# A batch of y in one 64 KB run per partition, with its last six rows copied aside so that its buffer comes free early

## The chip, the cores and the metric

The kernel runs on one core of one Trainium2 chip. The metric is the device time of one execution in microseconds (us); runs of the same kernel agree within about 0.3%. All comparisons below are of undisturbed ("fast") runs. Data travel in **packets**, here one per partition of a load, 8 on each of 16 DMA engines. A load **lands** when its semaphore says that all of it is there; landings are read from the start of the instruction that waits, about 0.1 us later, where nothing else is said. A **period** is the time from one batch's y to the next.

## The reference

```python
B, N, D = 8, 4096, 512
gram = np.matmul(x, y.transpose(0, 2, 1))
diag = np.diagonal(gram, axis1=1, axis2=2)      # only x[b,n,:] . y[b,n,:] is needed
diag = diag - diag.max(axis=-1, keepdims=True)
exp = np.exp(diag)
return (exp / exp.sum(axis=-1, keepdims=True)).astype(np.float32)
```

So it is 8 x 4096 dot products of 512 elements, then a softmax of each batch's 4096 results. Both inputs (134.22 MB together) are read once.

## The kernel before

A batch has 32 rows in each of 128 partitions (R = 32), 64 KB of x and 64 KB of y per partition. There are two buffers for x and one for y. SyncE ("SP") issues the loads in program order. VectorE multiplies in place and reduces. Batches 0 to 5 are "wide" (large instructions), batches 6 and 7 go row by row, because at the end short pieces shorten what follows the last load.

```python
xs = [big.tile([P, R, D], f32, name=f"xs{i}") for i in range(2)]
ys = big.tile([P, R, D], f32, name="ys")
# load_x / load_y: one DMA of n rows from r0 on.  dots_wide: xs *= ys (VectorE).
# sums_wide: diag[:, b, :] = sum of xs over D (VectorE).  dot_row: one row, multiply and sum.

for b in range(wide):                    # wide = 6
    load_x(b, 0, R)
    for r0 in (0, R // 2):
        load_y(b, r0, R // 2)
        dots_wide(b, r0, R // 2)
    ...                                  # softmax of batches 0 to 4 in between
    sums_wide(b)

b = B - 2
load_x(b, 0, R)
for r0 in (0, R // 2):
    load_y(b, r0, R // 2)
    for r in range(r0, r0 + R // 2):
        dot_row(b, r)

b = B - 1
r0 = 0
for n in (8, 8, 8, 4, 2, 1, 1):
    load_x(b, r0, n)
    load_y(b, r0, n)
    for r in range(r0, r0 + n):
        ...                              # softmax of batches 5 and 6 in between
        dot_row(b, r)
    r0 += n
last_softmax(b)
```

## Time and profile before

| | before |
|---|---|
| time, median | 322.69 us (4 runs, 322.57 to 322.77) |
| span in the profile | 320.5 us |
| load queue | 134.22 MB, 97.4% of 16 engines' span |
| VectorE busy | 78% |
| a wide batch | 38.78 us, of which VectorE works 34.60 |

From the page of the kernel before: the DMA row in 40 slices (9 is 90% busy or more), the packets, the load queue, the chain that ended last, and the three large groups of VectorE (busy us, mean ns of one | idle us before them, and what ended it).

```profile
span 320.5 us, 318 instructions
...
DMA  9999999899999999989999999999999999999991
...
DMA packets 6113, 134.36 MB, mean 419 GB/s; under 512 B 1632, under 2 KB 1632, under 8 KB 2400
...
q1 hardware_dynamic: 5040, 134.22, 97.4%
q10 hardware_dynamic: 1072, 0.13, 0.3%
q14 instruction: 1, 0.01, 0.0%
...
DMA 77%; DVE 20%; issue 1%; SPq 0%; POOLq 0%; ACT 0%; POOL 0%; DVEq 0%; ACTq 0%
...
L55 DVE TENSOR_TENSOR xs<-xs,ys 128x8192 f32<-128x8192 f32 x12 | 104.3, 8692 | 53.6 <-DMA ys<-in_y_dram 53.6
L58 DVE TENSOR_REDUCE diag<-xs 128x32 f32<-128x16384 f32 x6 | 103.3, 17220 | 0.2
L62 DVE SCALAR_TENSOR_TENSOR xs<-xs,ys 128x512 f32<-128x512 f32 x64 | 40.0, 688 | 13.8 <-DMA ys<-in_y_dram 13.6
```

The load queue is full from end to end. VectorE waits for y (53.6 + 13.6 us), and no slice but the last, with the final softmax, shows the queue empty. The 20% that the chain puts on VectorE ("DVE") is the time until a multiply releases the issue of a load; that load then stands behind others in the queue, so this is no cost unless the queue runs empty.

One wide period in the timeline (start, duration; "SPq" is the issue of a load by SyncE):

```profile
42.00 8.69 DVE L55 TENSOR_TENSOR xs<-xs,ys 128x8192 f32<-128x8192 f32 x1 [0.94 <-DMA ys<-in_y_dram]
50.73 17.22 DVE L58 TENSOR_REDUCE diag<-xs 128x32 f32<-128x16384 f32 x1
67.97 0.33 SPq L48 DMA_DIRECT2D xs<-in_x_dram  x1
71.13 8.69 DVE L55 TENSOR_TENSOR xs<-xs,ys 128x8192 f32<-128x8192 f32 x1 [3.19 <-DMA ys<-in_y_dram]
79.85 9.97 SPq L51 DMA_DIRECT2D ys<-in_y_dram  x2
80.77 8.69 DVE L55 TENSOR_TENSOR xs<-xs,ys 128x8192 f32<-128x8192 f32 x1 [0.95 <-DMA ys<-in_y_dram]
```

From 42.00 to 80.77 is 38.77 us for one batch of 16.78 MB, 433 GB/s. Note the **lead** of the x load: it is issued at 67.97, and the queue's earlier loads (y of the next batch) have landed by 80.77, so the load is queued 12.8 us before the queue would run out.

### The profile page before, as it was taken

What the parts mean: (1) busy time and instruction counts of PE and PEld (TensorE: products, weight loads), DVE (VectorE), ACT (ScalarE), POOL (GpSimd) and SP (SyncE); (2) the same over time, 40 slices, a digit from 0 to 9 for tenths busy, and PEclk for the clock granted to TensorE, in tenths of its full rate; (3) what the DMA queues carried; (4) which work ended last, traced back from release to release, by engine and by line L of the source; (5) the groups of instructions that cost most, each with busy time, mean ns of one, the idle gap of its engine ahead of it and who ended that gap; (6) DMA issues with size and microseconds to landing.
All of it is one profiled execution on the core that took longest, in us unless ns stands there. A gap on an engine that the chain in (4) does not pass through costs nothing.

```text
span 320.5 us, 318 instructions
## 1 busy us (share of the span) xinstructions
DVE 248.9 (78%) x154; ACT 6.2 (2%) x26; POOL 3.3 (1%) x10
## 2 busy tenths in 40 slices
DVE  0000989969999689996899968998789969994494
ACT  1000000000000000000000000000101000010000
POOL 0000000000000000000000000000000000000000
DMA  9999999899999999989999999999999999999991
GB/s 393 393 393 458 429 421 523 348 438 491 425 393 429 421 458 401 515 364 421 515 401 393 442 409 458 450 401 450 401 523 393 394 448 407 425 429 427 421 410 59
DMA packets 6113, 134.36 MB, mean 419 GB/s; under 512 B 1632, under 2 KB 1632, under 8 KB 2400
## 3 DMA queue, kind: packets, MB, share of 16 engines
q1 hardware_dynamic: 5040, 134.22, 97.4%
q10 hardware_dynamic: 1072, 0.13, 0.3%
q14 instruction: 1, 0.01, 0.0%
HBM read 134.22 MB, written 0.13 MB: 419 GB/s over the span
## 4 chain that ended last, share of the span: by engine, by line
DMA 77%; DVE 20%; issue 1%; SPq 0%; POOLq 0%; ACT 0%; POOL 0%; DVEq 0%; ACTq 0%
DMA ys<-in_y_dram 74%; DVE xs L55 16%; DVE xs L62 4%; DMA out_dram<-res 3%; SPq L48 0%; POOLq L162 0%; ACT res L91 0%; POOL lmx L98 0%; DVE res L103 0%; DVE lmxp L97 0%; DVE lrc L102 0%; DVEq L55 0%; DVE brc L88 0%; DVEq L62 0%; DVEq L103 0%
## 5 line engine op out<-in xcount | busy, mean ns | idle before, releaser
L55 DVE TENSOR_TENSOR xs<-xs,ys 128x8192 f32<-128x8192 f32 x12 | 104.3, 8692 | 53.6 <-DMA ys<-in_y_dram 53.6
L58 DVE TENSOR_REDUCE diag<-xs 128x32 f32<-128x16384 f32 x6 | 103.3, 17220 | 0.2
L62 DVE SCALAR_TENSOR_TENSOR xs<-xs,ys 128x512 f32<-128x512 f32 x64 | 40.0, 688 | 13.8 <-DMA ys<-in_y_dram 13.6
L62 DVE DVE_READ_ACCUMULATOR xs<-xs,ys 128x1 f32 x64 | 5.3, 83 | 0.0
L77 ACT ACTIVATE anmx<-amx 128x5 f32<-128x5 f32 x1 | 0.2, 208 | 221.9 <-POOL amx L76 221.9
L76 POOL PARTITION_ALL_REDUCE amx<-amxp x1 | 0.4, 386 | 223.1 <-DVE amxp L75 223.1
L79 ACT ACTIVATE res<-diag,anmx 128x32 f32<-128x32 f32 x5 | 1.5, 309 | 0.0
L91 ACT ACTIVATE res<-res,arc 128x32 f32<-128x32 f32 x5 | 1.2, 309 | 19.0 <-DVE arc L88 19.0
L76 POOL PARTITION_ALL_REDUCE bmx<-bmxp x1 | 0.7, 736 | 60.5 <-DVE bmxp L75 60.5
L77 ACT ACT_TABLE_LOAD x1 | 1.3, 1283 | 0.7 <-PEq L151 0.7
L77 ACT ACTIVATE bnmx<-bmx 128x2 f32<-128x2 f32 x1 | 0.2, 203 | 41.6 <-POOL bmx L76 41.6
L79 ACT ACTIVATION_READ_ACCUMULATOR res<-diag,anmx 128x1 f32 x5 | 0.9, 187 | 0.0
L102 DVE RECIPROCAL lrc<-lssum 128x1 f32<-128x1 f32 x1 | 0.2, 162 | 1.0 <-POOL lssum L101 1.0
L83 POOL PARTITION_ALL_REDUCE bssum<-bsump x1 | 0.8, 797 | 1.1 <-ACT res L79 1.1
L100 ACT ACTIVATE res<-diag,lnmx 128x32 f32<-128x32 f32 x1 | 0.3, 321 | 19.6 <-DVE lnmx L99 19.6
L91 ACT ACTIVATE res<-res,brc 128x32 f32<-128x32 f32 x2 | 0.5, 313 | 8.0 <-DVE brc L88 8.0
L98 POOL PARTITION_ALL_REDUCE lmx<-lmxp x1 | 0.4, 367 | 26.7 <-DVE lmxp L97 26.7
L79 ACT ACTIVATE res<-diag,bnmx 128x32 f32<-128x32 f32 x2 | 0.6, 314 | 0.0
L99 DVE TENSOR_SCALAR lnmx<-lmx 128x1 f32<-128x1 f32 x1 | 0.2, 153 | 0.5 <-POOL lmx L98 0.5
L83 POOL PARTITION_ALL_REDUCE assum<-asump x1 | 0.5, 459 | 2.0 <-ACT res L79 2.0
L101 POOL PARTITION_ALL_REDUCE lssum<-lsump x1 | 0.4, 397 | 0.7 <-ACT res L100 0.7
L79 ACT ACTIVATION_READ_ACCUMULATOR res<-diag,bnmx 128x1 f32 x2 | 0.4, 188 | 0.0
(11 smaller groups left out, 1.9 us busy)
## 6 DMA issues: line engine op xcount, KB each, us to landing
ys<-in_y_dram SPq DMA_DIRECT2D x14, 4096.0 KB, 30.0
xs<-in_x_dram SPq DMA_DIRECT2D x3, 2048.0 KB, 19.5
ys<-in_y_dram SPq DMA_DIRECT2D x3, 2048.0 KB, 19.9
xs<-in_x_dram SPq DMA_DIRECT2D x1, 1024.0 KB, 26.6
ys<-in_y_dram SPq DMA_DIRECT2D x1, 1024.0 KB, 27.0
xs<-in_x_dram SPq DMA_DIRECT2D x1, 512.0 KB, 25.9
ys<-in_y_dram SPq DMA_DIRECT2D x1, 512.0 KB, 22.2
xs<-in_x_dram SPq DMA_DIRECT2D x2, 256.0 KB, 12.4
```

The source lines that it names most:

```text
L55: nc.vector.tensor_tensor(out=xt, in0=xt, in1=ys[:, r0 : r0 + n, :], op=Alu.mult)
L58: nc.vector.tensor_reduce(out=diag[:, b, :], in_=xs[b % 2], axis=X, op=Alu.add)
L62: nc.vector.scalar_tensor_tensor(out=xt[:, r, :], in0=xt[:, r, :], scalar=1.0, in1=ys[:, r, :], op0=Alu.mult, op1=Alu.mult, accum_out=diag ...
L76: nc.gpsimd.partition_all_reduce(out_ap=mx, in_ap=mxp, channels=P, reduce_op=bass_isa.ReduceOp.max)
L77: nc.scalar.mul(nmx, mx, -1.0)
L79: nc.scalar.activation(out=res[:, b0 + i, :], in_=diag[:, b0 + i, :], func=Act.Exp, bias=nmx[:, i : i + 1], scale=1.0, accum_out=sump[:, i ...
L83: nc.gpsimd.partition_all_reduce(out_ap=ssum, in_ap=sump, channels=P, reduce_op=bass_isa.ReduceOp.add)
L91: nc.scalar.activation(out=rb, in_=rb, func=Act.Copy, scale=rc[:, i : i + 1])
L98: nc.gpsimd.partition_all_reduce(out_ap=mx, in_ap=mxp, channels=P, reduce_op=bass_isa.ReduceOp.max)
L99: nc.vector.tensor_single_scalar(out=nmx, in_=mx, scalar=-1.0, op=Alu.mult)
L100: nc.scalar.activation(out=rb, in_=db, func=Act.Exp, bias=nmx, scale=1.0, accum_out=sump)
L101: nc.gpsimd.partition_all_reduce(out_ap=ssum, in_ap=sump, channels=P, reduce_op=bass_isa.ReduceOp.add)
```

## The change

Its intent: y comes in one run of 64 KB per partition instead of two of 32 KB, as x does. With one buffer for y, this would leave the next y waiting until the whole multiply is done. So ScalarE, which is idle, copies the last 6 rows of y aside; the main multiply covers 26 rows and frees y's place; the last 6 rows are multiplied from the copy. The last batch begins with one piece of 16 rows instead of two of 8 (and of 8, then 4, 2, 1, 1).

```diff
+    K = 6
+    side = big.tile([P, K, D], f32, name="side")
...
     for b in range(wide):
         load_x(b, 0, R)
-        for r0 in (0, R // 2):
-            load_y(b, r0, R // 2)
-            dots_wide(b, r0, R // 2)
+        load_y(b, 0, R)
+        nc.scalar.activation(out=side, in_=ys[:, R - K :, :], func=Act.Copy)
+        dots_wide(b, 0, R - K, ys[:, : R - K, :])
+        dots_wide(b, R - K, K, side)
...
-    for n in (8, 8, 8, 4, 2, 1, 1):
+    for n in (16, 8, 4, 2, 1, 1):
```

(`dots_wide` takes its second operand as an argument now; `...` marks what is left out.)

More of the change, by code (lines that the diff above doesn't have):

```diff
@@ L51, in load_y, with dots_wide @@
         nc.sync.dma_start(out=ys[:, r0 : r0 + n, :], in_=yv[b, :, r0 : r0 + n, :])
-    def dots_wide(b, r0, n):
+    def dots_wide(b, r0, n, yt):
         xt = xs[b % 2][:, r0 : r0 + n, :]
-        nc.vector.tensor_tensor(out=xt, in0=xt, in1=ys[:, r0 : r0 + n, :], op=Alu.mult)
+        nc.vector.tensor_tensor(out=xt, in0=xt, in1=yt, op=Alu.mult)
     def sums_wide(b):
```

## The prediction

> **What bounds it now.** The load stream. The DMA table gives 134.22 MB, 97.4% of 16 engines' span. In the timeline y's second halves release VectorE at 80.77, 119.55 and 158.33 us: one batch (16.78 MB) per 38.78 us, 432.6 GB/s. The Trainium skill, "DMA: Bandwidth & Descriptors", section "Specifications", gives 435 GB/s as the fabric ceiling; the trace agrees within 1%. VectorE works 34.60 us of each period (table by stage): 4 us of slack. The chain of waits names VectorE's first multiply (16%) only because it releases the issue of a y load, which then stands in a queue that is never empty. Outside the stream: the first DMA is issued at 0.72 us, eight batches at the steady rate take 310.2 us, the last piece lands at 314.97, the last row, softmax and store end at 320.5.
>
> **What the change does.** Bytes stay the same.
> - Removed per wide batch: two multiplies of 128x8192 (8.69 us each) and two y issues. Added: one y issue, multiplies of 13312 and 3072 elements (estimates from 1.061 ns per element: 14.12 and 3.26 us). With the 17.22 us reduction VectorE needs 34.65 us, as before.
> - ScalarE copies 3072 elements: estimate 2.8 us, from the Trainium skill, "ScalarE: Activation LUTs" (0.28 us + 0.833 ns per element); no such copy is in the trace. It ends long before the 14.12 us multiply, which therefore frees y.
> - With T the landing of y: the next x (19.4 us of stream) is already queued and streams from T to T+19.4. The next y is issued at T+14.2, 5 us ahead of its turn; the x after it at T+34.7, when the reduction ends, 4 us ahead of T+38.8. At the start, issue to steady flow plus landing cost about 2.5 us (first half lands at 32.26, against 29.1 us of stream), so both leads suffice, but x's shrinks from 12.8 us to 4.
> - VectorE starts a batch only when all of y is there, the first at 42 us instead of 32. That is slack, until batch 6: its rows run from 271 to 290 instead of 265 to 285. The last batch's first piece (16 rows) lands at 294 and is done at 304.3, just after the 8 rows land (303.8); 4, 2, 1, 1 fit what is left. The last row again waits for its own landing.
> - The large result store lands at about 299 (before 286), the second at 308; the load that reuses its completion semaphore is issued then, ahead of its turn at 313.
>
> **Sum.** Head, stream and tail stay. Packet length is the uncertain term: a y half in 32 KB packets comes in 9.64 us (435 GB/s), x in 64 KB packets plus a y half in 29.14 us, so x in 19.50 (430). If 64 KB costs this, six batches lose 0.2 us each: +1.2 us. Fewer pieces at the end give back a few tenths. None of the change's gain lies on the critical path: the queue never ran dry.
>
> Predicted 322.8 us, range 321.9 to 324.2; faster by over 2%: 0.01; within 2%: 0.95; slower: 0.04.
>
> **What would show it.** Right: batch period 38.7 to 39.0 us; VectorE waits for y once per batch, about 4 us, in place of 3.2 + 0.95; last piece lands at 314 to 316; ScalarE's copies take about 2.8 us.
> Wrong: a period over 39.3 us, with empty DMA slices around the start of an x load; y's issue waiting for ScalarE; the last loads waiting for result stores; VectorE behind in the last pieces.
>
> **What would make it wrong.** A lead that really needs over 4 us costs some us per batch. A 64 KB y run that streams faster gains at most about 1.5 us, to the 435 ceiling.

## The result

| | before | after |
|---|---|---|
| time, median | 322.69 us (4 runs) | 322.15 us (4 runs, 321.98 to 322.44) |
| ratio of fast runs | | 0.9985, 95% interval 0.9967 to 1.0002 |
| span in the profile | 320.5 us | 320.3 us |
| wide batch | 38.78 us | 38.73 us |
| last y piece lands | 314.97 us | 314.76 us |

A ratio is the mean time of one kernel's fast runs over that of the other's of the same rounds, so it is not quite the ratio of the medians. The change moved the time by at most a few tenths of a microsecond. The wide batch is the mean distance of the multiplies that start when a whole y has landed: (235.69 - 42.02) / 5 after, (235.88 - 42.00) / 5 before. In these two traces the last landing moves by only 0.21 us, less than the medians of the runs do.

The same lines of the page after:

```profile
span 320.3 us, 310 instructions
...
DMA  9999999999999999999999999999999999999991
...
DMA packets 4961, 134.36 MB, mean 419 GB/s; under 512 B 1504, under 2 KB 1504, under 8 KB 2272
...
q1 hardware_dynamic: 3888, 134.22, 97.3%
...
DMA 60%; DVE 36%; issue 2%; SPq 0%; POOLq 0%; ACT 0%; POOL 0%; DVEq 0%; ACTq 0%
...
L58 DVE TENSOR_TENSOR xs<-xs,ys 128x13312 f32<-128x13312 f32 x6 | 84.2, 14025 | 62.6 <-DMA ys<-in_y_dram 62.6
L61 DVE TENSOR_REDUCE diag<-xs 128x32 f32<-128x16384 f32 x6 | 103.3, 17220 | 0.2
...
L112 ACT ACTIVATE side<-ys 128x3072 f32<-128x3072 f32 x6 | 16.6, 2763 | 185.3 <-DMA ys<-in_y_dram 185.3
L58 DVE TENSOR_TENSOR xs<-xs,side 128x3072 f32<-128x3072 f32 x6 | 20.1, 3352 | 0.0
```

and the period in the timeline after:

```profile
41.95 2.76 ACT L112 ACTIVATE side<-ys 128x3072 f32<-128x3072 f32 x1 [39.94 <-DMA ys<-in_y_dram]
42.02 14.02 DVE L58 TENSOR_TENSOR xs<-xs,ys 128x13312 f32<-128x13312 f32 x1 [42.02 <-DMA ys<-in_y_dram]
55.97 3.35 DVE L58 TENSOR_TENSOR xs<-xs,side 128x3072 f32<-128x3072 f32 x1
56.13 0.33 SPq L54 DMA_DIRECT2D ys<-in_y_dram  x1
59.35 17.22 DVE L61 TENSOR_REDUCE diag<-xs 128x32 f32<-128x16384 f32 x1
76.60 0.33 SPq L51 DMA_DIRECT2D xs<-in_x_dram  x1
80.73 14.03 DVE L58 TENSOR_TENSOR xs<-xs,ys 128x13312 f32<-128x13312 f32 x1 [4.16 <-DMA ys<-in_y_dram]
```

Three things are to be seen. The DMA row is full to the end as before, with 1152 packets fewer in the load queue (5040 to 3888). VectorE's share of the chain rose from 20% to 36% while the time did not move, which is what a share of that chain is worth when the queue is full. And the leads shrank: x is issued at 76.60 for a queue that runs out at 80.73, 4.1 us ahead instead of 12.8; y is issued 14.1 us after its predecessor landed, 5.2 us before x lands (at 61.3).

### The profile page after: what moved, and what is told of

Same layout as the page of the kernel before. It is cut to its first block, busy times and chain, and to the rows that moved or that the text cites. A ratio compares the mean times of both kernels' runs of the same rounds, so it can differ in the third digit from the quotient of the medians.

```text
span 320.3 us, 310 instructions
## 1 busy us (share of the span) xinstructions
DVE 247.8 (77%) x154; ACT 22.7 (7%) x32; POOL 3.3 (1%) x10
## 3 DMA queue, kind: packets, MB, share of 16 engines
q1 hardware_dynamic: 3888, 134.22, 97.3%
## 4 chain that ended last, share of the span: by engine, by line
DMA 60%; DVE 36%; issue 2%; SPq 0%; POOLq 0%; ACT 0%; POOL 0%; DVEq 0%; ACTq 0%
DMA ys<-in_y_dram 57%; DVE xs L58 27%; DVE xs L65 5%; DVE diag L61 4%; DMA out_dram<-res 3%; POOLq L166 0%; ACT res L94 0%; SPq L51 0%; POOL lmx L101 0%; DVE res L106 0%; DVE lmxp L100 0%; DVE lrc L105 0%; DVE bmxp L78 0%; SPq L54 0%; DVEq L58 0%
## 5 line engine op out<-in xcount | busy, mean ns | idle before, releaser
L58 DVE TENSOR_TENSOR xs<-xs,ys 128x13312 f32<-128x13312 f32 x6 | 84.2, 14025 | 62.6 <-DMA ys<-in_y_dram 62.6
L112 ACT ACTIVATE side<-ys 128x3072 f32<-128x3072 f32 x6 | 16.6, 2763 | 185.3 <-DMA ys<-in_y_dram 185.3
L58 DVE TENSOR_TENSOR xs<-xs,side 128x3072 f32<-128x3072 f32 x6 | 20.1, 3352 | 0.0
```

What stands on the lines that cost most here:

```text
L58: nc.vector.tensor_tensor(out=xt, in0=xt, in1=yt, op=Alu.mult)
L112: nc.scalar.activation(out=side, in_=ys[:, R - K :, :], func=Act.Copy)
```

## The experiments

The theories that were put against each other:

- **A**: the load stream bounds; the change saves only the fixed part of packets.
- **B**: the early freeing of y is a gain, given back by VectorE's later start at the end.
- **C**: the leads matter; without the copy, or with less lead, loads would come too late. The prediction had put the need at about 2.5 us; before the first runs I lowered this to 1.5 us.
- **D**: packet length costs nothing.
- **E**: instruction fetches of VectorE share the load's engines and cost time.
- **F** and **G**, formed after the second set: a lead of about 2.5 us is enough (F), or any shortening costs in proportion (G).

| run | what differs | median us | ratio to before |
|---|---|---|---|
| e1_y_run_only | wide part of the change alone | 322.19 | 0.9982 |
| e2_pieces_only | last batch's pieces alone | 322.58 | 0.9997 |
| e3_no_side | changed, no copy aside | 331.53 | 1.0289 |
| e4_short_packets | changed, 16 KB packets | 324.58 | 1.0060 |
| e5_short_reduce | changed, most of the reduction cut | 321.80 | 0.9983 |
| e6_lead_2us | changed, x about 2.1 us ahead | 329.50 | 1.0229 |
| e7_lead_1us | changed, x about 1.0 us ahead | 328.36 | 1.0186 |
| e9_more_instr | changed, 256 tiny instructions more | 324.54 | 1.0066 |
| e10_lead_3us | changed, x about 3.1 us ahead | 325.71 | 1.0096 |
| e11_old_plus3us | before, 3.3 us more of VectorE | 322.54 | 1.0002 |
| e12_copy_2_rows | changed, 2 rows aside | 329.05 | 1.0188 |
| e13_one_memset | control for e9 | 322.19 | 0.9990 |

Before had medians of 322.68, 322.57 and 322.51 us in the three sets (e1 to e4, e5 to e9, e10 to e13). All results but that of e5 were correct. By the rule of 2% only e3 and e6 count as slower, and e7 and e12 are unclear; that all four are slower than before is clear of noise (the lowest of their intervals begins at 1.0136).

### The two halves of the change

e1 takes the changed kernel with the old pieces:

```diff
-    for n in (16, 8, 4, 2, 1, 1):
+    for n in (8, 8, 8, 4, 2, 1, 1):
```

> The wide batches as changed (y in one run, ScalarE's copy), the last batch in the old pieces 8, 8, 8, 4, 2, 1, 1. Theory A (the load stream bounds; the change saves only the fixed time of packets, about 8 to 9 ns each: a 32 KB packet takes 1213 ns and a 64 KB one 2418 in the traces, 2 x 1213 - 2418 = 8): each engine has 48 packets of 64 fewer, so 322.2 to 322.4, 0.3 to 0.5 us under before. Rival B (a gain of the early y is given back by VectorE's later start at the end): this run, which keeps the small first pieces, is under 321.8.

Measured: 322.19 us, ratio 0.9982 (0.9970 to 0.9994). e2 is the kernel before with the new pieces:

```diff
-    for n in (8, 8, 8, 4, 2, 1, 1):
+    for n in (16, 8, 4, 2, 1, 1):
```

> The old wide batches, the last batch in pieces 16, 8, 4, 2, 1, 1. Theory A: 16 packets per engine fewer, 322.5 to 322.7, at most 0.2 us under before. Rival B: over 323, because the larger first piece lets VectorE begin the last batch later.

Measured: 322.58 us, ratio 0.9997 (0.9985 to 1.0009). The small gain sits in the wide batches, the pieces are worth nothing measurable, and neither run shows a gain that the other part gives back: B falls.

### Packet length

e4 loads x and y of the wide batches of the changed kernel in pieces of 8 rows:

```diff
-        load_x(b, 0, R)
-        load_y(b, 0, R)
+        for r0 in range(0, R, 8):
+            load_x(b, r0, 8)
+        for r0 in range(0, R, 8):
+            load_y(b, r0, 8)
```

> The changed kernel with x and y of the wide batches loaded in pieces of 8 rows (16 KB packets) instead of whole: 64 packets per engine and batch instead of 16, six more loads per batch. Theory A at 8 to 9 ns a packet: 288 packets more per engine in six batches = 2.3 to 2.6 us, plus 0.3 us of completion packets (36 more of 9 ns): 324.6 to 325.2. Rival D (packet length costs nothing, the half us is something else, such as fewer loads or waits): 322.1 to 322.6.

Measured: 324.58 us (324.45 to 324.85), 2.4 us over the changed kernel; the period is 39.16 us instead of 38.73. That is at the lower end of what A gave, and D falls. In the packet records of the traces a packet takes 611 ns at 16 KB, 1213 at 32 KB and 2418 at 64 KB (medians): the time is proportional to the bytes, plus 8 to 9 ns (2 x 1213 - 2418 = 8, 2 x 611 - 1213 = 9). This also sizes the change itself. Each engine has 64 data packets fewer (4480 to 3456 in all, over 16) and 8 completion packets of 9 ns fewer; 64 x 8 + 8 x 9 ns = 0.6 us. The medians differ by 0.54 us. As the interval of the direct comparison includes 1, the gain itself rests on e1's interval and on this sum.

### Does VectorE's part cost anything?

e5 cuts the wide reductions to 32 of 512 elements per row:

```diff
-        nc.vector.tensor_reduce(out=diag[:, b, :], in_=xs[b % 2], axis=X, op=Alu.add)
+        nc.vector.tensor_reduce(out=diag[:, b, :], in_=xs[b % 2][:, :, 0:32], axis=X, op=Alu.add)
```

> The changed kernel with the wide reductions cut to 32 of 512 elements per row (a wrong result on purpose): about 16 us of VectorE's 34.6 us per batch are gone, and x is issued some 16 us earlier. Theory A (stream bounds, VectorE's 27% in the chain of waits is no cost): 321.9 to 322.3, unchanged. Rival C (the late issue of x, 4 us ahead, costs time): at least 1 us faster.

Measured: 321.80 us, ratio 0.9983 (0.9968 to 0.9998), where the changed kernel has 0.9985. From its timeline:

```profile
59.45 1.22 DVE L61 TENSOR_REDUCE diag<-xs 128x32 f32<-128x1024 f32 x1
60.69 0.33 SPq L51 DMA_DIRECT2D xs<-in_x_dram  x1
...
80.82 14.03 DVE L58 TENSOR_TENSOR xs<-xs,ys 128x13312 f32<-128x13312 f32 x1 [20.15 <-DMA ys<-in_y_dram]
```

VectorE is rid of 16 us of work per batch and waits 20 us for y; x is issued 20 us ahead, and y lands when it always did. So the stream is the bound, and the 4.1 us of lead that the changed kernel leaves lose nothing that can be measured.

### How much lead a load needs

e3 leaves the copy out; one multiply of 32 rows frees y's place:

```diff
-        nc.scalar.activation(out=side, in_=ys[:, R - K :, :], func=Act.Copy)
-        dots_wide(b, 0, R - K, ys[:, : R - K, :])
-        dots_wide(b, R - K, K, side)
+        dots_wide(b, 0, R, ys)
```

> y in one run but no copy aside: one multiply of 128x16384 from y, which frees y's place at about T+17.3 instead of T+14.1 (T: landing of y), 2 us before its turn by landing times. Theory A with a need of about 1.5 us[...]: no loss, 322.1 to 322.3, so the copy buys nothing. Rival C (the need is the 2.5 us of the prediction or more, and the copy is what makes the long run bearable): 0.5 us or more per batch lost, 325 or more.

Measured: 331.53 us (330.27 to 333.98), 9.4 us over the changed kernel. My lowered need of 1.5 us was plainly wrong. (In the changed kernel the first packet starts 1.0 us after the first issue, 0.72 to 1.71, and the landing comes 0.35 us after the last engine is done, 22.25 to 22.60.) The DMA row of its page, and its timeline:

```profile
DMA  9899998999997989989998998999999999999991
```

```profile
42.06 17.23 DVE L58 TENSOR_TENSOR xs<-xs,ys 128x16384 f32<-128x16384 f32 x1 [42.06 <-DMA ys<-in_y_dram]
59.32 0.33 SPq L54 DMA_DIRECT2D ys<-in_y_dram  x1
...
83.19 17.23 DVE L58 TENSOR_TENSOR xs<-xs,ys 128x16384 f32<-128x16384 f32 x1 [6.64 <-DMA ys<-in_y_dram]
```

y is issued 17.3 us after the landing instead of 14.1, 2.0 us before x lands (61.3), and the next y comes after 41.13 us instead of 38.71: 2.4 us lost in this batch. The DMA row has 7 slices at 8 or 7, where the changed kernel has only 9s up to the last slice and the kernel before has 2 such.

e6 and e7 shorten the lead of x instead. They add VectorE work that nobody needs before the reduction (4 or 6 rows of the copy, 2.2 or 3.3 us), which only moves the issue of x back; VectorE still fits in the period.

```diff
+    spare = small.tile([P, K], f32, name="spare")
...
         dots_wide(b, R - K, K, side)
+        nc.vector.tensor_reduce(out=spare[:, 0:4], in_=side[:, 0:4, :], axis=X, op=Alu.add)
```

(e7 has 6 in place of 4, e10 below has 2; both have the same `spare`.)

> The changed kernel with one more VectorE reduction of 2048 elements (about 2.2 us) before the reduction of each wide batch: x is issued about 1.9 us before its turn by landing times instead of 4.1. Theory A with a need of about 1.5 us: 322.1 to 322.4, unchanged. Rival C (need of 2.5 us, as the prediction had it): about 0.5 us per batch, six batches: 325.

> The same with 3072 elements (about 3.3 us): x is issued about 0.8 us before its turn. Theory A with a need of 1.5 us: 0.6 to 0.7 us per batch are lost in six x loads, so 325.5 to 326.5, and the batch period grows from 38.73 to 39.4. With a need under 0.8 us: unchanged.

Measured: 329.50 us (327.81 to 330.31) and 328.36 us (326.92 to 330.39). e6 loses far more than the 0 of A and also more than the 2.5 us of C; e7 loses more than expected too, in another rhythm. In e7's trace the periods are 38.69, 40.32, 38.69, 40.32, 38.73 us; in e6's 38.70, 39.85, 38.72, 40.94, 38.76. A period that slips gives the next x more lead, because VectorE's issue stays while the landing comes later; so every second batch recovers. By the packet records the queue really runs dry: in e7 no load packet at all is in flight (begun and not ended) from 80.1 to 80.5 us, in e6 only 11 are at 80.2 (16, one for each engine, is full). The first packets afterwards take up to 1.2 us longer than the 2.42 us of a packet in a full stream.

One thing in them tells against a fixed need: in recovered periods, leads of 2.6 us (e7, twice) and 3.2 us (e6, 117.29 to 120.50) lost nothing. From e7's timeline:

```profile
118.27 0.33 SPq L52 DMA_DIRECT2D xs<-in_x_dram  x1
120.88 14.02 DVE L59 TENSOR_TENSOR xs<-xs,ys 128x13312 f32<-128x13312 f32 x1 [2.64 <-DMA ys<-in_y_dram]
...
159.57 14.03 DVE L59 TENSOR_TENSOR xs<-xs,ys 128x13312 f32<-128x13312 f32 x1 [1.01 <-DMA ys<-in_y_dram]
```

The next y comes 38.69 us after 120.88, as in an undisturbed period. From these four runs I took 2.5 us to be the need (F), and tested a lead of about 3 us:

```diff
         dots_wide(b, R - K, K, side)
+        nc.vector.tensor_reduce(out=spare[:, 0:2], in_=side[:, 0:2, :], axis=X, op=Alu.add)
```

> The changed kernel with one more VectorE reduction of 1024 elements (about 1.2 us) per wide batch: x is issued about 3.0 us before y's landing instead of 4.1. Theory F (a load must be issued about 2.5 us before the last landing, since the 16 engines run dry one by one; in the traces of the runs with 2.2 and 3.3 us of extra work, leads of 2.06 to 2.11 and 0.98 us lost 1.1 to 2.2 us and leads of 2.6 and 3.2 lost none): unchanged, 322.1 to 322.6. Rival G (any shortening of the lead costs in proportion): about 325.

Measured: 325.71 us (324.30 to 326.70), 3.6 us over the changed kernel. F falls. G, as I had put it, named about 325, but the losses are not in proportion: leads of 3.1, 2.1 and 1.0 us, where the changed kernel has 4.1, cost 3.6, 7.4 and 6.2 us against its 322.15. From e10's timeline:

```profile
77.47 0.33 SPq L52 DMA_DIRECT2D xs<-in_x_dram  x1
...
80.61 14.03 DVE L59 TENSOR_TENSOR xs<-xs,ys 128x13312 f32<-128x13312 f32 x1 [3.16 <-DMA ys<-in_y_dram]
...
116.19 0.33 SPq L52 DMA_DIRECT2D xs<-in_x_dram  x1
...
119.36 14.02 DVE L59 TENSOR_TENSOR xs<-xs,ys 128x13312 f32<-128x13312 f32 x1 [3.20 <-DMA ys<-in_y_dram]
...
159.27 14.02 DVE L59 TENSOR_TENSOR xs<-xs,ys 128x13312 f32<-128x13312 f32 x1 [4.36 <-DMA ys<-in_y_dram]
```

A lead of 3.14 us (77.47 to 80.61) lost nothing: the next y landed 38.75 us later, at 119.36. A lead of 3.17 us (116.19 to 119.36) lost 1.2 us: 159.27 is 39.91 later. A third, of 3.09 us (194.84 to 197.93), lost 2.4. So at 3.1 us it is chance, and at 4.1 to 4.2 us none of the changed kernel's x loads in the wide part was late. Its x load of the last batch, issued at 270.27 and 4.2 us ahead, was a little: at 273.65 us only 9 load packets are in flight, where e5, which issues it at 254.21, has 15 or 16. What decides between late and not late shows in the last experiment.

e12 does the same for y's lead, with a copy of 2 rows:

```diff
-    K = 6
+    K = 2
```

> The changed kernel with 2 rows copied aside instead of 6: the main multiply is 30 rows, about 16.1 us, and y is issued about 3.2 us before x's landing (6 rows: 5.2; none: 2.1, which cost 9 us). Theory F: unchanged, 322.1 to 322.8. If y's load needs more lead than x's: 324 or more.

Measured: 329.05 us (327.19 to 329.40). y is issued 16.2 us after its predecessor landed, 3.0 us before x lands (58.31, 61.3), and that is too late as well; the periods are 39.16, 41.09, 38.85, 40.73 and 39.10 us. So the copy is no decoration: without it, or with a third of it, the single run of y costs 7 to 9 us.

e11 is the counter-check on the kernel before, with 3.3 us more VectorE work per wide batch, as in e7:

```diff
+    idle = big.tile([P, 6, D], f32, name="idle")     # zeroed once by GpSimd; spare: [P, 6]
...
             dots_wide(b, r0, R // 2)
+        nc.vector.tensor_reduce(out=spare, in_=idle, axis=X, op=Alu.add)
```

> The kernel before, with the same extra 3.3 us of VectorE per wide batch that cost the changed kernel 6 us. Theory F: its x is issued 12.8 us ahead, so 9.5 are left; VectorE needs 38.0 of 38.78 us; unchanged, 322.6 to 323.1. If the loss came from VectorE's load itself and not from the lead: 326 or more.

Measured: 322.54 us, ratio 1.0002 (0.9987 to 1.0017).

```profile
89.52 3.35 DVE L114 TENSOR_REDUCE spare<-idle 128x6 f32<-128x3072 f32 x1
92.78 17.21 DVE L61 TENSOR_REDUCE diag<-xs 128x32 f32<-128x16384 f32 x1
110.02 0.33 SPq L51 DMA_DIRECT2D xs<-in_x_dram  x1
110.05 8.69 DVE L58 TENSOR_TENSOR xs<-xs,ys 128x8192 f32<-128x8192 f32 x1
...
119.70 8.69 DVE L58 TENSOR_TENSOR xs<-xs,ys 128x8192 f32<-128x8192 f32 x1 [0.96 <-DMA ys<-in_y_dram]
```

x is issued 9.7 us ahead (110.02 to 119.70), and the same extra work that cost the changed kernel 6 us costs nothing here. VectorE's load was never the matter; the lead is.

### Instruction fetches

Both kernels' traces have one 8 KB packet of the instruction queue ("q14") near row 10 of batch 6. The 32 KB load packet that follows it took 1.7 to 1.8 us instead of 1.2, and the last 7 or 8 packets of the stream follow one another in steps of 0.08 us, as those of one engine would, and end 0.5 to 0.65 us after the others. e9 puts more fetches in, with 256 tiny writes while VectorE waits for the first load:

```diff
+    spare = small.tile([P, K], f32, name="spare")
...
+    for i in range(256):
+        nc.vector.memset(spare[:, i % K : i % K + 1], 0.0)
```

> The changed kernel with 256 tiny VectorE memsets at the start, while it waits for the first loads (under 42 us). In the traces of both kernels one 8 KB packet of the instruction queue falls about 10 rows into batch 6, beside a 32 KB load packet that took 1.8 us instead of 1.2, and the last packets come from one lagging engine alone, about 0.6 us after the rest. Theory E: an instruction fetch sets one engine back and the end waits for that engine. More fetches: if they fall on the same engine, the last landing comes 0.5 us later per further fetch; 322.6 to 323.8. Otherwise unchanged, 322.1 to 322.3.

Measured: 324.54 us (323.97 to 325.46), 2.4 us over the changed kernel, more than expected.

The instruction queue on its page, and the writes in its timeline:

```profile
q14 instruction: 3, 0.02, 0.0%
```

```profile
0.80 1.75 DVE L111 MEMSET spare<- 128x1 f32 x61 [0.80 <-PEq L159]
...
2.92 3.63 DVE L111 MEMSET spare<- 128x1 f32 x128 [0.37 <-DVE spare L111]
9.26 1.92 DVE L111 MEMSET spare<- 128x1 f32 x67 [2.70 <-issue]
...
43.71 14.03 DVE L59 TENSOR_TENSOR xs<-xs,ys 128x13312 f32<-128x13312 f32 x1 [32.54 <-DMA ys<-in_y_dram]
```

VectorE stops after 61 writes and again 128 later, the second time for 2.7 us, waiting for nothing that the profile shows; the two new 8 KB packets fall at 7.48 and 13.15 us. The first y lands 1.7 us later than in the changed kernel (43.71 against 42.02). Then something follows that was not expected: the next x is issued at 78.29 for a landing at 82.49, a lead of 4.2 us as in the changed kernel, but by the packet records as few as 10 load packets are in flight between 80.1 and 81.4 us, and the following y comes 39.93 us after the last.

e13 is the control, four large writes instead:

```diff
+    for i in range(4):
+        nc.vector.memset(side, 0.0)
```

> Control for the 256 small memsets: 4 large memsets of VectorE at the start, some 6 to 13 us of its time in all, without further instruction fetches. Theory E (the fetches cost, 2.4 us there): 322.1 to 322.5, and the first y lands at about 42.0 us as in the changed kernel, not 43.7. If VectorE's writes during the first loads cost: about 324.

Measured: 322.19 us (322.09 to 322.29), the first y at 42.17 us. So VectorE's writes cost nothing; the many instructions do. My explanation was that a fetch holds one engine back, and that the other 15 then run dry before the landing that I measure leads from.

The traces do not name the engine of a packet, but their times show most of this. Each load leaves 16 completion packets of 4 bytes; I take them as one from each engine when its share is done. In e9's first load 15 of them come from 21.65 to 22.47 us and the last at 23.80; in e13 all 16 come from 21.72 to 22.39. The late one is the engine of both fetches, for there each packet begins within 12 ns of the end of the one before: fetch (7.48, 0.31 us), load packet (7.78, 2.95 instead of 2.42 us), load packet (10.73), fetch (13.15, 0.33 us), load packet (13.47, 3.08 us), and so on to the completion packet at 23.80. The first y's landing is this engine's. So x, issued at 78.29, is 4.1 us ahead of y's landing (82.40) but only 1.8 us ahead of the first engine that is done (80.05). In the changed kernel this second distance is 3.0 to 3.1 us for the x loads of the wide part.

The same count sorts the other runs. In the ten traces of changed kernels with whole loads (all but e4), 84 loads of the wide part were issued less than 7 us before the landing. By the distance to the first engine that is done, all 54 with 2.8 us or more cost at most 0.35 us, all 9 with less than 1 us cost more than that, and of the 21 between, 11 did. (The cost is how much later than 19.35 us after its predecessor a load is done, by the mean or by the last of its engines, whichever is more.) It fits e10, too: its three x loads with about 3.1 us to the landing had 2.3, 2.2 and 1.2 us to the first engine, and lost 0, 1.2 and 2.4 us. But this is a count over traces, not a run made to test it, and it gives no sharp need: three loads at 1.4 to 1.7 us (e6, e7) lost nothing, and why stays open.

## Why the prediction was right

The measured 322.15 us lies in the range of 321.9 to 324.2, and "within 2%" had 0.95. Point by point:

- **"The load stream" bounds: right.** e5 shows it most directly: with 16 us less VectorE work per batch, y lands at the same times.
- **VectorE's work unchanged: right.** 14.02 + 3.35 + 17.22 us, where 14.12, 3.26 and 17.22 were written.
- **ScalarE's copy 2.8 us: right** (2.763), ending long before the multiply that frees y. The Trainium skill, "ScalarE: Activation LUTs", section "What ACT_TABLE_LOAD costs", gives 186 ns + 0.833 ns per element for immediate scale and bias, 2745 ns for 3072 elements, and the trace agrees with 2763. The prediction used the form with a pointer operand, 2839 ns.
- **"Both leads suffice": right in the outcome, wrong in the size of the need, and so in part luck.** The need was put at about 2.5 us, from the first load of the kernel, which starts into idle engines, and was held against the landing, which is that of the slowest engine. In the full stream 3.1 to 3.2 us were too little in two of three cases of e10, and 4.1 us was enough in the changed kernel but not in e9. The changed kernel passes with at most 1 us to spare, as e10 shows, not with the 1.6 us that the prediction believed. Its last paragraph, that a need of over 4 us would cost some us per batch, was the right worry.
- **"If 64 KB costs this": wrong.** This term raised the forecast over the time before. The prediction took a landing distance of 9.64 us for half of y and of 29.14 us for x plus half of y, and concluded that x in 64 KB packets is slower (430 against 435 GB/s). Packet durations say the contrary: 8 packets of 1213 ns are 9.70 us and 8 of 2418 ns are 19.34 us. The rate is the same, and one long packet is 8 ns cheaper than two short ones. Distances between landings of neighbouring loads are too coarse for a difference of 1%. In its place stands a saving of 0.6 us, as sized under e4; so the forecast of 322.8 lay just above the time before, and the measured time just below it.
- **"None of the change's gain lies on the critical path": nearly.** Freeing y earlier gained nothing by itself, as said; the smaller number of packets, on the stream itself, gained about half a microsecond.
- **The end: right.** The last piece landed at 314.76 us (314 to 316 was said), and the last row waited for its own landing. The first store landed at 299.0, as said, the second at 310.05 against 308 forecast; the load that waited for the second was issued at 310.12, and the last landing was no later than before.

No experiment pointed to a version that beats both kernels by more than a few tenths of a microsecond: even with 20 us of lead (e5) the time falls by 0.35 us in the medians, and the ratio to before stays the same within noise (0.9983 against 0.9985).

## What to carry to other kernels

When the load queue is full all the time, ask of a change to the buffers not how much sooner a buffer comes free, but how far ahead of the queue's end each load is still issued; in these runs more lead was worth nothing once it was long enough, and a late load cost as much as 2.4 us (e10). Count the lead to the first engine that runs out of work, not only to the landing, which is that of the slowest: e9's load was 4.1 us ahead of the one and 1.8 us of the other. Here the changed kernel is as fast as the old one but works at most 1 us from that edge; 3.3 us of extra work cost it 6 us and the old one nothing. That is the same time in a table, but not the same robustness against a later edit. And before blaming a size of packets, read the durations of the packets, not the distances between landings.

## What the Trainium skill lacked or had wrong

- "DMA: Bandwidth & Descriptors", sections "Latency and other measured facts" (a first byte after about 600 ns for a load issued by SyncE; here the first packet starts 1.0 us after the first issue begins) and "Two cost components" under "Anatomy of one DMA" (about 2.0 us fixed, measured on the other issue path, which no run here uses): no page says how far ahead of a full queue's end a load must be issued. Here 3.1 to 3.2 us before the last landing was too late in two of three cases of e10 and 2.6 to 3.2 us was not in three cases of e6 and e7; 4.1 us was enough in the changed kernel and too late in e9. Counted to the first engine that is done, 2.8 us or more cost at most 0.35 us. A late load cost 1.2 to 2.4 us in e10.
- The same page, section "Rules for kernel authors", asks for DMAs of at least 1 MiB for the most bandwidth, which no run here tests. It gives no cost for the run per partition above that size: 2 MB loads with 16 KB packets cost 2.4 us against 8 MB loads with 64 KB packets (e4), 8 to 9 ns per packet.
- "Runtime: NRT & Kernel Launch", section "Instruction fetch mechanics", gives refills in blocks of 16 KiB (256 instructions), at a cost "mostly hidden". The traces show 8 KB packets and VectorE stopping 128 instructions apart, once for 2.7 us; two more such fetches in a full load stream came with 1.7 us at the first landing and 2.4 us at the end (e9, against e13).
